# GLA's decayed queries by one product and a spread over heads on Pool, and matmul operands at multiples of 512 bytes

## Chip, core and metric

The kernel runs on one core of a Trainium2 chip. The metric is the device time of one execution in microseconds, the median of several runs. PE is TensorE (PEld its weight load), DVE VectorE, ACT ScalarE, POOL GpSimd and SP the engine whose queue issues the DMAs.

## What is computed

One step of a streaming encoder layer in float32: 64 tokens of a running stream, 16 learned meta tokens and 2048 new tokens, model width 1024. The reference, cut:

```
h = rms_norm(x);  proj = h @ w_in
aq, ak, av, lx, lg, gq, gk, gv, glr, gog = split(proj)
o = concat[diff_attention(aq, ak, av), rg_lru(lx, lg), gla(gq, gk, gv, glr, gog)] @ w_out;  x = x + o
h = rms_norm(x);  x = x + (gelu(causal_dwconv3(h @ w_up)) * (h @ w_gate)) @ w_down
y = rms_norm(x)
```

The gated linear attention (GLA) has 4 heads with 32 key and 64 value channels. In blocks of tokens it needs, for every pair i >= j of a block,

```
att[i, j] = sum_d q[i, d] * k[j, d] * exp(b[i, d] - b[j, d])        # b: running sum of the log gates
```

## The kernel before

**Products.** The big products run as three float32r products: operand and weight are each split into a rounded part and a remainder (h, l), and hi·hi, lo·hi and hi·lo are summed in PSUM. So a product over 1024 rows is 8 k steps of three matmuls, 24 in all. A weight piece is a tile of 128x1024: DMA'd into `raw` (two buffers), rounded by ACT into `whi` (L151), the remainder `wlo` made by Pool (L257) for two in three and by DVE (L157) for the rest (three buffers of each); the split pieces are stored in HBM (`WS`) and loaded again by later groups.

**Stages.** A tile scheduler orders each engine's instructions by its own simulated times and by priorities that the code sets; a generator that yields costs (`yield 800`) is one strand, and `flow` weaves the strands. Up to about 2035 us these strands run woven: `win` (the input projection over six blocks of columns, up to 384 tokens each; L641 with weights standing, L643 with tokens standing), `attention` (scores L1052 and L1059, row maximum `NB` on DVE L1061, exp `pc` on ACT L1062, mixing on Pool L154 and DVE L1100, transposes L1151, values L1166), `recurrent` (the RG-LRU and GLA, chunk by chunk: first the 64 + 16 tokens, then eight chunks of 256), and the first two FFN groups of 512 columns. From about 1888 us the second FFN group is alone. Stage three, from about 2035 us, is the third FFN group with column blocks of 336, 256 and 512: the output projection (L1434), `up_gate` (products `pu` and `pg`, L1299, for 22 tiles of the hidden width), and `down` (`pd`, L1366) after every four tiles, a "quad".

**A GLA level.** Within a block of 128 tokens the decay matrix is built in levels of half lengths m = 64, 32, ..., 1 (`level(li, m)`, seven a chunk, six in the first: 62). Per level, for all 128 key channels of the four heads by n = 256 tokens (128 in the first chunk): DVE makes the exponents in the tile EK (L878, L879), ACT the exp (L880, written E in the code), Pool the decayed keys kl = k * E in the second half of EK (L882), and DVE the decayed queries of the second halves (L886): four products of 32 channels by 128 tokens, each into its head's block of the block diagonal tile BD (128 x 4 x 128). There are two BD tiles per chunk, zeroed by Pool when the chunk starts (L864) and used in turn. PE multiplies kl by BD for each of the chunk's two groups of 128 tokens (L891), DVE copies the result under a mask into `att` (L895). `att` starts as the diagonal, set by Pool (L154, att<-ident,dg). EK, BD and other working tiles come from one ring of nine tiles of 2 KB (`rc`, NRC = 9).

**Addresses.** Offsets in bytes of a partition: the weight tiles lie at 16928, 21024 and 25120 (`whi`) and 29216, 33312 and 37408 (`wlo`), each 32 past a multiple of 512. The token tiles of `win` and of FFN groups 0 and 1 also lie 32 past a multiple of 512 (h2h of group 0 at 41504). In stage three the H tiles lie 480 past one: h2h of the 336-column block at 158688, of 256 columns at 180192, of 512 columns at 196576. One k step of H is 4n bytes, 1344 for n = 336. A gated tile `gh` or `gl` holds the three blocks one after the other, 1104 columns, 4416 bytes; their starts lie at odd multiples of 32.

The matmul of L1299, with H on the moving side and the weights standing:

```
for k in range(KT):
    for i3, (wi_, hx) in enumerate(((0, hk), (0, lk), (1, hk))):
        nc.tensor.matmul(ps[:, :n], lhsT=w_[wi_][:, k * P:(k + 1) * P], rhs=hx, ...)
```

Of the kernel before, what the change touches and what calls it, by code (L numbers as in the profile page):

```python
# [21 lines left out]
P = 128  # L22
# [113 lines left out]
def tile_hymba_step(ctx, tc, xT, xkT, cache_v, wi, wo, wu, wg, wd, par, sgla, c_msk, yT_p, yT_s, nkT_p, nv_p, lh_p, lc_p, gs_p, fc_p,  # L136
# [61 lines left out]
    lrue = cst.tile([P, 16], F32, name="lrue")  # L198
    halo = cst.tile([P, NF, 2], F32, name="halo")
    fce = cst.tile([P, 2, 2, NF], F32, name="fce")  # L200

    def pr(name, i=0, n=1):
        a = PAR[name][0] + i
# [579 lines left out]
    def gla(c):  # L783
# [75 lines left out]
        yield 1200  # L859

        att = [rc("att", (P, 4, P)) for _ in range(nb)]
        Bs = [rc("BD", (P, 4, P)) for _ in range(2)]
        for B_ in Bs:
            nc.gpsimd.memset(B_[:, :, :n // 2], 0.0)  # L864
        for j in range(nb):
            for h in range(4):
                pool_scaled(att[j][:, h, :], ident, dg[:, j, h:h + 1])
# [1 line left out]

        def level(li, m):  # L870
            cn = n // (2 * m)
            B_ = Bs[li % 2]
            bv = b[:, :n].rearrange("p (c t) -> p c t", t=2 * m)
            EK = rc("EK")
            E, kl = EK[:, 0, :], EK[:, 1, :]
            ew = E[:, :n].rearrange("p (c t) -> p c t", t=2 * m)
            ref = bv[:, :, m - 1:m].to_broadcast([P, cn, m])
            nc.vector.tensor_tensor(ew[:, :, 0:m], ref, bv[:, :, 0:m], ALU.subtract)  # L878
            nc.vector.tensor_tensor(ew[:, :, m:], bv[:, :, m:], ref, ALU.subtract)  # L879
            nc.scalar.activation(out=E[:, :n], in_=E[:, :n], func=AF.Exp, scale=1.0 / 16)  # L880
            yield 800
            nc.gpsimd.tensor_tensor(out=kl[:, :n], in0=k[:, :n], in1=E[:, :n], op=ALU.mult)  # L882
            qv = q[:, :n].rearrange("p (c t) -> p c t", t=2 * m)
            for h in range(4):
                r = slice(32 * h, 32 * h + 32)
                nc.vector.tensor_tensor(B_[r, h, :n // 2].rearrange("p (c t) -> p c t", t=m), qv[r, :, m:], ew[r, :, m:],  # L886
                                        ALU.mult)
            yield 800
            for j in range(nb):
                ps = half_bank().rearrange("p (h c) -> p h c", c=64)  # L890
                nc.tensor.matmul(ps, lhsT=kl[:, j * P:(j + 1) * P], rhs=B_[:, :, j * 64:(j + 1) * 64], start=True, stop=True)  # L891
                cc = P // (2 * m)
                ov = att[j].rearrange("p h (c t) -> p h c t", t=2 * m)[:, :, :, m:]
                mv = msk[:, li, :].rearrange("p (o c t) -> p o c t", o=1, t=m).to_broadcast([P, 4, cc, m])
                nc.vector.copy_predicated(out=ov, mask=mv, data=ps.rearrange("p h (c t) -> p h c t", t=m))  # L895
                yield 500
# [361 lines left out]
    def open3():  # L1258
        env["hs"].close()
        env["dg"], env["rg"] = "dg", "rg"  # L1260
        env["ps"] = p2.enter_context(tc.tile_pool(name="ps_x", bufs=5, space=PSUM))

        env["hp"] = p2.enter_context(tc.tile_pool(name="hp3", bufs=1, side="right"))
        env["xp"] = [p2.enter_context(tc.tile_pool(name="xp3", bufs=4, side="right")),
                     p2.enter_context(tc.tile_pool(name="xp4", bufs=4))]
        env["ev"] = p2.enter_context(tc.tile_pool(name="ev3", bufs=2))
        env["gp"] = p2.enter_context(tc.tile_pool(name="gp3", bufs=5))

    x2 = {}
# [6 lines left out]
    def up_gate(g, ff, H, gt, norms):  # L1276
        (wu_,), (wg_,) = w_take(("up", g, ff), 1), w_take(("gate", g, ff), 1)
        ev2, gp = env["ev"], env["gp"]
        gw = sum(FGROUPS[g])
        gh = gp.tile([P, gw], F32R, tag="gh", name="gh")  # L1280
        gl = gp.tile([P, gw], F32R, tag="gl", name="gl")
        gt[ff] = (gh, gl)
        cw = [pr("fcw", 22 * w + ff) for w in range(3)]
        cb = pr("fcb", ff)
        goff = 0
        for bi, n in enumerate(FGROUPS[g]):
            yield from norms.pop(bi, ())
            us = []
            for a, b, kind in ffn_pieces(g, n):
# [42 lines left out]
            for a, b, kind, uh, cc in us:  # L1332
# [5 lines left out]
                gh_, gl_ = gh[:, goff + a:goff + b], gl[:, goff + a:goff + b]  # L1338
                pool_scaled(gh_, cc[:, :m])
                minus(gl_, cc[:, :m], f(gh_))  # L1340
            goff += n
        w_used(2)

    def offsets(g):
        return [sum(FGROUPS[g][:b]) for b in range(len(FGROUPS[g]))]

    def down(g, q, gt, done=None, outs={}):
# [8 lines left out]
        for i, (ct, b) in enumerate(order):  # L1356
            half = ct // 4
            if half not in W:
                W[half] = w_take(("down", g, q, half), len(gts) // 2)
            o, n = offsets(g)[b], FGROUPS[g][b]  # L1360
            ps = env["ps"].tile([P, NMAX], F32, tag="w", name="pd")
            for j, (gh, gl) in enumerate(gts):
                c = j % 2 * NMAX + ct % 4 * P
                wh, wl = (a[:, c:c + P] for a in W[half][j // 2])
                for i3, (g_, w_) in enumerate(((gh, wh), (gh, wl), (gl, wh))):
                    nc.tensor.matmul(ps[:, :n], lhsT=w_, rhs=g_[:, o:o + n], start=(j == 0 and i3 == 0),  # L1366
                                     stop=(j == len(gts) - 1 and i3 == 2))
                if j % 2:
                    w_pump()
                    yield 6 * n * 0.425  # L1370
                    yield from beside(outs)
            nc.vector.tensor_tensor(x2[b, ct], x2[b, ct], ps[:, :n], ALU.add)  # L1372
            if done:
                done(b, ct)
            if all(c // 4 != half for c, _ in order[i + 1:]):
                w_used(len(gts) // 2)
# [258 lines left out]
```

## Time and profile before

| what | value |
|---|---|
| median of 3 runs | 2956.35 us (2955.74 to 2959.2) |
| profiled execution | 2957.12 us, its span 2955.3 us |
| PE busy | 2841.2 us, 96% |
| DVE busy | 1890.9 us, 64% |
| ACT busy | 1138.1 us, 39% |
| POOL busy | 870.5 us, 29% |
| mean granted clock of PE | 0.982 |

A matmul is in the trace with its modelled end, so the time that one takes in a stream is read from start to start, or from the chain of work, which gives runs of matmuls of one line as one piece. The shares are means over very unlike stretches; the windows tell them apart.

### The profile page before, as it was taken

Reading aid. Unit: us, or ns where it says so; the run is one execution under the profiler, and the core shown is the slowest. Engines: PE = TensorE matmul, PEld = TensorE weight load, DVE = VectorE, ACT = ScalarE, POOL = GpSimd, SP = SyncE. Lnnn points to the kernel's source line nnn. Section 1 sums busy time; section 2 is a strip of 40 time slices with the busy share of each in tenths; the row PEclk is TensorE's granted clock in tenths of the full one; section 3 lists DMA queues with packets and bytes.
Section 4 is the critical chain, followed back from the end, with each engine's and each line's share of the span. In section 5 each row is a group of like instructions: output and inputs, shape, how many; then the busy total and the mean of one; then the engine's idle time right before and its main releaser. Section 6 shows DMA issues by size and latency. Waiting matters only on the chain.

```text
span 2955.3 us, 44538 instructions
## 1 busy us (share of the span) xinstructions
PE 2841.2 (96%) x16031; PEld 2508.7 (85%) x16031; DVE 1890.9 (64%) x3699; ACT 1138.1 (39%) x2589; POOL 870.5 (29%) x1212
## 2 busy tenths in 40 slices
PE   7999999999898998999999999999999999999997
PEld 7988899989876887787787888888989998999997
DVE  7677685778879879879969865333454333333335
ACT  5354554555555454545445433211222121212122
POOL 4435534434535445444424221000110000000001
PEclk9999999999999999999999999999999999999999
DMA  7675564656796776777875565685222222222222
GB/s 241 201 217 148 179 214 139 199 179 186 227 338 212 252 264 234 249 266 261 285 258 183 197 203 183 208 327 186 72 86 86 86 86 86 86 86 86 86 86 105
DMA packets 277930, 537.43 MB, mean 182 GB/s; under 512 B 31014, under 2 KB 170030, under 8 KB 277710
## 3 DMA queue, kind: packets, MB, share of 16 engines
q1 hardware_dynamic: 277566, 534.58, 54.9%
q8 instruction: 127, 2.08, 0.3%
q14 instruction: 93, 0.76, 0.1%
q10 hardware_dynamic: 144, 0.01, 0.0%
HBM read 382.74 MB, written 151.76 MB: 181 GB/s over the span
## 4 chain that ended last, share of the span: by engine, by line
PE 69%; DVE 14%; DMA 4%; issue 2%; ACT 2%; POOL 1%; SPq 0%; POOLq 0%; ACTq 0%; DVEq 0%
PE pd L1366 15%; PE pg L1299 14%; PE pu L1299 14%; PE pd L1434 6%; PE ps_w L641 5%; PE ps_w L643 3%; DVE pc L1100 3%; PE ps_o L1166 3%; PE ps_sc L1059 2%; PE ps_pt L1151 2%; PE ps_sc L1052 2%; DVE BD L886 1%; DVE NB L1061 1%; PE ps_r L891 1%; DVE y L435 1%
## 5 line engine op out<-in xcount | busy, mean ns | idle before, releaser
L257 POOL TENSOR_TENSOR wlo<-raw,whi 128x1024 fp32r<-128x1024 f32 (+1 forms) x104 | 249.8, 2404 | 309.6 <-ACT whi L151 278.5
L1062 ACT ACTIVATE pc<-ps_sc,NB 128x512 f32<-128x512 f32 (+6 forms) x400 | 224.5, 562 | 298.2 <-DVE NB L1061 262.6
L1299 PE MATMUL pu<-h2h,whi 128*128 128x512 f32 (+2 forms) x880 | 316.8, 360 | 5.0 <-ACT h2h L151 2.8
L1323 DVE SCALAR_TENSOR_TENSOR cc<-uh,prm,cc 128x512 f32<-128x512 f32 (+4 forms) x264 | 165.0, 634 | 242.9 <-ACT cc L1321 239.8
L1299 PE MATMUL pu<-h2l,whi 128*128 128x512 f32 (+2 forms) x880 | 316.2, 359 | 1.4 <-DVE h2l L157 1.4
L1299 PE MATMUL pu<-h2h,wlo 128*128 128x512 f32 (+2 forms) x880 | 316.5, 360 | 0.0
L1366 PE MATMUL pd<-gh,whi 128*128 128x512 f32 (+2 forms) x880 | 314.2, 360 | 2.1 <-DMA whi<-WS 1.4
L1299 PE MATMUL pg<-h2h,wlo 128*128 128x512 f32 (+2 forms) x880 | 315.6, 359 | 0.4 <-DMA wlo<-WS 0.4
L1299 PE MATMUL pg<-h2l,whi 128*128 128x512 f32 (+2 forms) x880 | 315.9, 359 | 0.0
L1299 PE MATMUL pg<-h2h,whi 128*128 128x512 f32 (+2 forms) x880 | 315.0, 358 | 0.7 <-DMA whi<-WS 0.5
L1366 PE MATMUL pd<-gh,wlo 128*128 128x512 f32 (+2 forms) x880 | 314.5, 358 | 0.0
L1366 PE MATMUL pd<-gl,whi 128*128 128x512 f32 (+2 forms) x880 | 312.9, 357 | 0.0
L1372 DVE TENSOR_TENSOR x<-x,pd 128x512 f32<-128x512 f32 (+2 forms) x240 | 141.8, 595 | 217.1 <-PE pd L1366 216.1
L641 PE MATMUL ps_w<-hh,whi 128*128 128x384 f32 (+2 forms) x768 | 259.1, 340 | 16.0 <-ACT whi L151 10.5
L1316 ACT ACTIVATE uh<-pu 128x336 f32<-128x336 f32 (+3 forms) x132 | 59.3, 464 | 539.6 <-PE pu L1299 539.1
L1061 DVE TENSOR_REDUCE NB<-ps_sc 128x1 f32<-128x512 f32 (+6 forms) x400 | 209.5, 529 | 86.8 <-PE ps_sc L1059 85.2
L641 PE MATMUL ps_w<-hl,whi 128*128 128x384 f32 (+2 forms) x768 | 259.6, 339 | 0.4 <-DVE hl L157 0.4
L641 PE MATMUL ps_w<-hh,wlo 128*128 128x384 f32 (+2 forms) x768 | 256.0, 335 | 0.3 <-DVE wlo L157 0.3
L154 POOL TENSOR_SCALAR gh<-cc 128x336 fp32r<-128x336 f32 (+3 forms) x132 | 72.9, 553 | 444.8 <-DVE cc L1336 440.0
L151 ACT ACTIVATE whi<-raw 128x1024 fp32r<-128x1024 f32 (+2 forms) x160 | 165.8, 1036 | 96.7 <-DMA raw<-in_wi 30.5
L1299 PEld LDWEIGHTS pu<-h2h,whi 128*128 128x128 f32 x880 | 167.4, 190 | 26.6 <-ACT h2h L151 3.2
L154 POOL TENSOR_SCALAR pc<-pc,fr 128x512 f32<-128x512 f32 (+4 forms) x200 | 156.8, 802 | 109.3 <-DVE fr L1082 86.1
(330 smaller groups left out, 7142.5 us busy)
## 6 DMA issues: line engine op xcount, KB each, us to landing
whi<-WS SPq DMA_DIRECT2D x148, 512.0 KB, 4.3
wlo<-WS SPq DMA_DIRECT2D x148, 512.0 KB, 4.3
raw<-in_wi SPq DMA_DIRECT2D x74, 512.0 KB, 4.1
WS<-whi SPq DMA_DIRECT2D x74, 512.0 KB, 3.1
WS<-wlo SPq DMA_DIRECT2D x74, 512.0 KB, 6.0
Kc<-KHL SPq DMA_DIRECT2D x48, 512.0 KB, 5.8
V<-VHL SPq DMA_DIRECT2D x48, 512.0 KB, 3.5
Q<-QHL SPq DMA_DIRECT2D x64, 256.0 KB, 4.4
```

What stands on the lines that cost most here:

```text
L151: nc.scalar.activation(out=out, in_=in_, func=AF.Copy, scale=scale)
L154: nc.gpsimd.tensor_scalar(out, in_, s, 1.0, ALU.mult, ALU.mult)
L257: nc.gpsimd.tensor_tensor(out=lo[:, :n], in0=t[:, :n], in1=f(hi[:, :n]), op=ALU.subtract)
L641: nc.tensor.matmul(ps[:, :n], lhsT=wx, rhs=hx, start=st_, stop=sp_)
L643: nc.tensor.matmul(ps[:n, :wd_], lhsT=hx, rhs=wx, start=st_, stop=sp_)
L1061: nc.vector.tensor_reduce(NB[:qw, ti, m, ci:ci + 1], ps[:qw, :kt_], AX.X, ALU.min)
L1062: nc.scalar.activation(out=pv_[m][:qw, :kt_], in_=ps[:qw, :kt_], func=AF.Exp, scale=-1.0, bias=NB[:qw, ti, m, ci:ci + 1], accum_out=SS[:qw ...
L1299: nc.tensor.matmul(ps[:, :n], lhsT=w_[wi_][:, k * P:(k + 1) * P], rhs=hx, start=(k == 0 and i3 == 0), stop=(k == KT - 1 and i3 == 2))
L1323: nc.vector.scalar_tensor_tensor(out=cc[:, :m], in0=uh[:, w:w + m], scalar=cw[w], in1=cc[:, :m], op0=ALU.mult, op1=ALU.add)
L1366: nc.tensor.matmul(ps[:, :n], lhsT=w_, rhs=g_[:, o:o + n], start=(j == 0 and i3 == 0), stop=(j == len(gts) - 1 and i3 == 2))
L1372: nc.vector.tensor_tensor(x2[b, ct], x2[b, ct], ps[:, :n], ALU.add)
L1434: nc.tensor.matmul(ps[:, :n], lhsT=w_, rhs=g_, start=(k == 0 and i3 == 0), stop=(k == KT - 1 and i3 == 2))
```

## The change

**GLA levels.** The two BD tiles of a chunk and their zeroing go. Each level takes two more tiles from the `rc` ring: `qe`, the decayed queries of all 128 channels by 128 tokens in one DVE product, and BD, which Pool writes whole: qe, repeated over the four heads, times the head indicator of the channel (`hind`, four columns of `prm`), 128x512 with the zeros among it. EK's lines shift by three: L878 is now L875, L879 L876, L882 L879, L886 becomes L883 (DVE) and L886 (Pool), L891 L890; L257 is L258.

**Addresses.** A tile of 480 bytes (`pad0`) in front of the weights moves them and what lies behind by 480: weights and the H tiles of FFN groups 0 and 1 then begin at multiples of 512. In stage three a pad of 480 bytes on the right side brings the three H pairs to multiples of 512 (158208, 179712, 196096 for h2h), and one of 64 on the left with gated tiles of 1152 columns does it for gh and gl; `places` puts their blocks largest first at multiples of 128 columns (512 at 0, 336 at 512, 256 at 896). Of the 336-column H only each eighth k step lies at a multiple of 512, as 1344 is none.

```diff
+    nc.gpsimd.memset(cst.tile([P, 120], F32, name="pad0"), 0.0)
...
         att = [rc("att", (P, 4, P)) for _ in range(nb)]
-        Bs = [rc("BD", (P, 4, P)) for _ in range(2)]
-        for B_ in Bs:
-            nc.gpsimd.memset(B_[:, :, :n // 2], 0.0)
...
-            B_ = Bs[li % 2]
...
             nc.gpsimd.tensor_tensor(out=kl[:, :n], in0=k[:, :n], in1=E[:, :n], op=ALU.mult)
             qv = q[:, :n].rearrange("p (c t) -> p c t", t=2 * m)
-            for h in range(4):
-                r = slice(32 * h, 32 * h + 32)
-                nc.vector.tensor_tensor(B_[r, h, :n // 2].rearrange("p (c t) -> p c t", t=m), qv[r, :, m:], ew[r, :, m:],
-                                        ALU.mult)
+
+            qe, B_ = rc("qe", (P, P))[:, :n // 2], rc("BD", (P, 4, P))
+            nc.vector.tensor_tensor(qe.rearrange("p (c t) -> p c t", t=m), qv[:, :, m:], ew[:, :, m:], ALU.mult)
+            qb = qe.rearrange("p (o c) -> p o c", o=1).to_broadcast([P, 4, n // 2])
+            hb = pr("hind", 0, 4).rearrange("p (h o) -> p h o", o=1).to_broadcast([P, 4, n // 2])
+            nc.gpsimd.tensor_tensor(out=B_[:, :, :n // 2], in0=qb, in1=hb, op=ALU.mult)
             yield 800
...
+        pad(p2.enter_context(tc.tile_pool(name="pad_r", bufs=1, side="right")), 480)
         env["hp"] = p2.enter_context(tc.tile_pool(name="hp3", bufs=1, side="right"))
...
+        pad(p2.enter_context(tc.tile_pool(name="pad_l", bufs=1)), 64)
         env["gp"] = p2.enter_context(tc.tile_pool(name="gp3", bufs=5))
...
-        gw = sum(FGROUPS[g])
+        at, gw = places(g)
...
-        goff = 0
         for bi, n in enumerate(FGROUPS[g]):
+            goff = at[bi]
...
-            goff += n
         w_used(2)
+
+    def places(g):
+
+        at, n = {}, 0
+        for b in sorted(range(len(FGROUPS[g])), key=lambda b: -FGROUPS[g][b]):
+            at[b] = n
+            n += -(-FGROUPS[g][b] // P) * P
+        return at, n
+
+    def pad(pool, n):
+        nc.gpsimd.memset(pool.tile([P, n // 4], F32, tag="pad", name="pad", bufs=1), 0.0)
...
-            o, n = offsets(g)[b], FGROUPS[g][b]
+            o, n = places(g)[0][b], FGROUPS[g][b]
```

**Order.** The scheduler weaves the part up to stage three anew: PE carries out the same matmuls, some 5000 of them at another place, the level's matmuls at most some 60 places away. From stage three's first `down` product on PE's order is the same. On Pool, where the seventh chunk's levels begin, the order before was (the line of each instruction, its operation, output<-inputs, partitions x elements; uh, fce and halo belong to the FFN's convolution):

```order
L154 TENSOR_SCALAR att<-ident,dg 128x128 x8
L882 TENSOR_TENSOR EK<-qk,EK 128x256 x2
L257 TENSOR_TENSOR wlo<-raw,whi 128x1024
L882 TENSOR_TENSOR EK<-qk,EK 128x256
L257 TENSOR_TENSOR wlo<-raw,whi 128x1024
L1318 COPY fce<-uh 128x2
L1320 COPY halo<-uh 128x2
L882 TENSOR_TENSOR EK<-qk,EK 128x256
```

Now, on Pool at the same place (pc<-pc,fr scales attention's exponentials):

```order
L154 TENSOR_SCALAR att<-ident,dg 128x128 x8
L879 TENSOR_TENSOR EK<-qk,EK 128x256
L258 TENSOR_TENSOR wlo<-raw,whi 128x1024
L154 TENSOR_SCALAR pc<-pc,fr 128x512 x4
L154 TENSOR_SCALAR pc<-pc,fr 128x384 x2
L154 TENSOR_SCALAR pc<-pc,fr 128x16
L154 TENSOR_SCALAR pc<-pc,fr 128x144
L886 TENSOR_TENSOR BD<-qe,prm 128x512
L879 TENSOR_TENSOR EK<-qk,EK 128x256
L258 TENSOR_TENSOR wlo<-raw,whi 128x1024
L1319 COPY fce<-uh 128x2
L1321 COPY halo<-uh 128x2
```

Between the first level's kl and its BD there are now a weight split and eight scalings; the second level's kl comes behind that BD.

On DVE, where the fifth chunk's levels begin (738 us in the trace of before), the order before was (NB is the row maximum of attention, pl a remainder of its probabilities, msk the level's mask):

```order
L878 TENSOR_TENSOR EK<-bl 128x2x64
L879 TENSOR_TENSOR EK<-bl 128x2x64
L878 TENSOR_TENSOR EK<-bl 128x4x32
L879 TENSOR_TENSOR EK<-bl 128x4x32
L886 TENSOR_TENSOR BD<-qk,EK 32x128 x8
L1061 TENSOR_REDUCE NB<-ps_sc 128x1 x2
L157 TENSOR_TENSOR pl<-ps_pt,ph 128x512
L895 COPY_PREDICATED att<-msk,ps_r 128x4x64
```

Now, on DVE at the same place:

```order
L875 TENSOR_TENSOR EK<-bl 128x2x64
L876 TENSOR_TENSOR EK<-bl 128x2x64
L883 TENSOR_TENSOR qe<-qk,EK 128x128
L875 TENSOR_TENSOR EK<-bl 128x4x32
L876 TENSOR_TENSOR EK<-bl 128x4x32
L1060 TENSOR_REDUCE NB<-ps_sc 128x1 x2
L157 TENSOR_TENSOR pl<-ps_pt,ph 128x256
L883 TENSOR_TENSOR qe<-qk,EK 128x128
L1060 TENSOR_REDUCE NB<-ps_sc 128x1 x2
L157 TENSOR_TENSOR pl<-ps_pt,ph 16x256
L894 COPY_PREDICATED att<-msk,ps_r 128x4x64
```

The eight products of two levels have become two, each behind its own level's exponents, with attention's row maxima between them.

## Rows read from the trace of the kernel before

**Rows 1.** Windows: busy time of each engine by stretch; first row: columns.

```profile
core 0: us, PE busy (x) PEld busy (x) DVE busy (x) ACT busy (x) POOL busy (x), PEclk, DMA share, GB/s
...
100.00:900.00 800.00, 758.18 (x4831) 703.55 (x4830) 603.80 (x1236) 408.24 (x1020) 334.11 (x378) 0.98 0.66 203
900.00:1888.00 988.00, 954.33 (x4740) 788.17 (x4739) 790.44 (x1540) 462.82 (x1077) 381.83 (x507) 0.98 0.69 231
...
2146.00:2938.00 792.00, 790.42 (x4670) 718.36 (x4670) 315.50 (x570) 158.01 (x287) 65.83 (x202) 1.00 0.24 85
```

**Rows 2.** Waits: who waited <- releaser: us in total, times, longest us.

```profile
PE ps_sc L1052 <- ACT pc L1062: 22.4, 24, 3.5
...
PE ps_r L891 <- POOL EK L882: 0.4, 1, 0.4
PE ps_r L891 <- DVE BD L886: 0.4, 1, 0.4
...
ACT pc L1062 <- DVE NB L1061: 262.6, 174, 8.1
```

**Rows 3.** Chain of work, FFN group 1 alone: start us, us, what, matmuls.

```profile
1902.77 5.44 PE pu L1299 x24
```

**Rows 4.** Chain of work, stage three, 2146 to 2890 us.

```profile
2172.00 5.60 PE pu L1299 x24
...
2183.20 3.71 PE pu L1299 x24
...
2193.35 2.72 PE pg L1299 x24
...
2262.79 2.83 PE pu L1299 x24
...
2474.25 33.38 PE pd L1366 x204
...
2507.78 14.84 PE pd L1366 x84
```

**Rows 5.** Chain of work, projection stage, 440 to 480 us.

```profile
447.47 4.16 PE ps_w L641 x24
```

**Rows 6.** Groups by line and shape: out<-in, xcount | busy us, mean ns | idle before.

```profile
L257 POOL TENSOR_TENSOR wlo<-raw,whi 128x1024 fp32r<-128x1024 f32 x96 | 234.7, 2446 | 297.5 <-ACT whi L151 270.4 <-PE ps_w L643 7.4 <-issue 7.2
L886 DVE TENSOR_TENSOR BD<-qk,EK 32x128 f32<-32x128 f32 x224 | 104.0, 464 | 8.3 <-ACT EK L880 5.6
L154 POOL TENSOR_SCALAR pc<-pc,fr 128x512 f32<-128x512 f32 x96 | 85.4, 906 | 73.7 <-DVE fr L1082 71.2 <-PE ps_w L641 1.3 <-DVE dg L858 1.0
...
L879 DVE TENSOR_TENSOR EK<-bl 128x128 f32<-128x128 f32 x56 | 19.0, 340 | 0.0
...
L740 POOL TENSOR_TENSOR rc<-rc,sq 128x512 f32<-128x512 f32 x8 | 11.7, 1468 | 50.9 <-DVE tt L738 25.6 <-ACT lgt L749 16.2 <-issue 7.3
L940 POOL TENSOR_TENSOR oS<-oS,gss 128x512 f32<-128x512 f32 x8 | 8.8, 1097 | 0.5
...
L886 DVE TENSOR_TENSOR BD<-qk,EK 32x64 f32<-32x64 f32 x24 | 6.6, 275 | 1.7 <-ACT EK L880 1.3
```

**Rows 7.** All instructions of L886: duration ns min/median/max, first and last start.

```profile
L886 DVE TENSOR_TENSOR BD<-qk,EK x248: 212/288/2489, 100.0 to 1683.2; 32x128 f32<-32x128 f32 x112, 32x64 f32<-32x64 f32 x12
```

**Rows 8.** Timeline, a first and an ordinary level: start us, us, engine, what.

```profile
741.02 1.44 POOL L882 TENSOR_TENSOR EK<-qk,EK 128x256 f32<-128x256 f32 x2
741.84 0.70 PE L891 MATMUL ps_r<-BD,EK 128*128 128x256 f32 x2 [0.36 <-POOL EK L882]
...
1432.66 1.62 DVE L886 TENSOR_TENSOR BD<-qk,EK 32x128 f32<-32x128 f32 x4
1432.71 0.83 POOL L882 TENSOR_TENSOR EK<-qk,EK 128x256 f32<-128x256 f32 x1 [2.88 <-ACT EK L880]
...
1446.49 0.59 PE L891 MATMUL ps_r<-BD,EK 128*128 128x256 f32 x2
```

## Prediction

> **What bounds the kernel now.** I read the windows by stage first. Two kinds of stretch stand apart [rows 1]. From 2146 to 2938 us PE is busy for 790.4 of 792 us at a granted clock of 1.00, DVE for 40% and Pool for 8%: there the time is the number of matmuls times their spacing, and nothing that DVE or Pool does can show. From 100 to 1888 us (input projection, attention and recurrence woven with the first FFN groups) PE stands still for 41.8 + 33.7 = 75.5 us while DVE is busy for 603.8 + 790.4 = 1394.2 us, 78%. So the change has to be judged twice: by spacing in stage three, by waiting before it.
>
> The list of waits says whose fault the idle time of the mixed part is [rows 2]: the longest entry of PE is 22.4 us ahead of attention scores, for a bank that ACT's exp (L1062) frees; ACT in turn waited 262.6 us for DVE's row maximum (L1061). So DVE's load is felt, but thinly. The level that the change rewrites barely shows: PE waited once, 0.4 us, for BD and once, 0.4 us, for kl.
>
> Then the chain of work, for the spacing. All big products here are 24 matmuls, eight k steps by three splits. In FFN group 1 alone (1888 to 2035 us) a 512-column product takes 5.44 us [rows 3], 226.7 ns a matmul; 14 of 15 such rows say 5.44. In stage three the same code with the same 512 columns takes 5.60 us, 233.4 ns (36 rows of 5.60, three each of 5.59 and 5.61) [rows 4]. Clock and shape are the same. What differs in the program is where the operands lie: in group 1 H and weights both begin 32 bytes past a multiple of 512, in stage three the 512-column H begins 480 past one and the weights 32 past. The 256-column products, also at 480 against 32, take 2.83 us in 35 of 41 rows and 2.72 us in the other six, so 113.3 ns can be had there too, and it is half of 226.7: I call these two the floor. By columns the floor of 336 is 226.7 x 336/512 = 148.8 ns, 3.57 us a product; the row says 3.71. Against the address as the cause speaks the projection stage: H and weights both 32 past a multiple, and a 384-column product takes 4.16 us [rows 5] where the floor is 226.7 x 384/512 x 24 = 4.08.
>
> **The change, part by part.** The sum is made against the profiled execution's 2957.12 us; the median of the runs is 0.8 us lower.
>
> *Addresses in stage three.* After the change H of the 512- and 256-column blocks, the weights and the start of each gh and gl block lie on multiples of 512. 512 columns: 22 tiles of up and gate are 44 products, and the output projection has 8 more, 52 x (5.60 - 5.44) = 8.3 us. 256 columns: 44 products of which 35 in 41 are slow, 44 x 35/41 x 0.11 = 4.1 us. 336 columns: each k step is 1344 bytes on, so seven of eight H operands stay off a multiple; I take 0, with 44 x 0.14 = 6.2 us as the other end. Down: a full quad is 33.38 + 14.84 = 48.22 us for 288 matmuls [rows 4]; at the floor it is 96 x 1104/512 x 226.7 ns = 46.9 us, so 1.3 us by 5.5 quads, 7.2 us at most. Its old gh addresses ran over all odd multiples of 32, some of them as the weights', and I saw no faster quads there; I take half, 3.6, ends 0 and 7.2. Together 16.0 us, ends 0 (the address does nothing) and 25.8. A loss in this part has nothing to rest on: PE's order from the first down product of stage three on is the same and no operand gets further from a multiple.
>
> The Trainium skill ("TensorE: Matmul & The Clock Gate", Back-to-back issue gap) gives the spacing at full clock as columns over 2.4 GHz plus about 2.5 ns, 216 for 512, with no term for where an operand lies. By that rule this part is worth 0 and the first rival holds. The trace disagrees at least on the size: 226.7 and 233.4 ns for one shape at one clock [rows 3, 4].
>
> *Addresses before stage three.* FFN groups 0 and 1 go from 32 against 32 to 0 against 0; attention's operands don't move. I take 0. If the win products fell to the floor, 64 of 384 columns would give 64 x 0.08 = 5 us.
>
> *DVE.* Out go 224 products of 32x128 and 24 of 32x64, 104.0 + 6.6 = 110.6 us [rows 6]. In come 56 of 128x128, 340 ns by L879's row, and six of half the size at about half, 20.0 us; L886's 464 ns against 340 for four times the rows also shows that a DVE product costs by columns, not partitions. Net -90.6 us, 6.5% of 1394.2. The same share of 75.5 us of PE idle is 4.9, I take 5. Ends: the whole of the 22.4 us that PE waits for exp as the gain, and a loss of 12 us from the next item.
>
> *Pool.* Out go 18 memsets. In come 62 products, BD from qe and the head columns, 56 of them 128x512: between 1.10 us (L940, also with a broadcast operand) and 1.47 (L740) [rows 6], 65 to 87 us with the six of half the size; I take the first, nearest in shape. Pool was busy 334.1 + 381.8 of 1788 us, 40%, and goes to about 44%: room, but in a queue that runs in order. Each level now runs exp, then DVE's qe beside Pool's kl (0.83 us), then BD on Pool, where DVE made BD in 1.62 us beside kl [rows 8]. So BD is ready 0.83 + 1.10 - 1.62 = 0.3 us later, and more where something stands between kl and BD on Pool: nothing in 24 of 62 levels; a wlo split (2.45 us) alone or with scalings of attention in most others; in the seventh chunk's first level, quoted above, a split and eight scalings, 2.45 + 4 x 0.91 + about 1.7 by columns for the other four = 8 us. Queued behind BD on Pool are the next kl, wlo (for which the projection's third split waits) and the scalings of attention. Cover: in an ordinary level BD was ready at 1434.28 us and its matmul ran at 1446.49, 12.2 us later. In a chunk's first level Pool's two kl end at 742.46 and PE's two matmuls at 742.54; nothing covers it. Of the eight first levels behind the first chunk's, five have nothing or a two-column copy on Pool in between (0.3 us each), the last two a gh scaling (about 1 us each), the seventh chunk's the 8: about 12 us, if PE stands for all of it, which is the loss above. The three pad memsets stand at tile set-up, away from PE's chain. The BD and qe tiles come from the rc ring of nine, three a level where one was: a level's tiles must be free before the third next begins, which the order on DVE gives anyway; 0.
>
> The Trainium skill ("SBUF — State Buffer", SBUF: two separate sides) says that DVE with two SBUF inputs and GpSimd lock one port pair for a whole instruction and that the loser blocks. The trace agrees: one BD product took 2489 ns where the median is 288 [rows 7], about one wlo split. By that rule 62 new Pool holds of 1.1 us would block DVE for up to 68 us and eat most of its 90; the mixed term would be 1 in place of 5 and the time 2940.
>
> *Sum:* 2957.1 - 16.0 - 5 = 2936 us; with the address worth between half of it, 8, and all, 25.8, it is 2944 to 2926.
>
> **Rivals.**
> *B, the address does nothing*, and 5.44 against 5.60 is something else that sets in with stage three (the 256-column products change between 2.72 and 2.83 at unchanged addresses, and 384 columns miss the floor when aligned: both speak for it; against it, that nearly all 512-column rows of a place agree to 0.01 us, as a fixed cause would make them). Only DVE's 5 us stay: 2952.
> *C, every product falls to the floor*, 336 columns and all of down too, since the weights count by themselves: 25.8 + 5 in the projection + 5 = 35.8, 2921. For it: all shapes of stage three are above the floor by much the same 5 to 7 ns, 336 too, whose addresses vary. Against: rows 5.
> *D, slower: Pool becomes what PE waits for in each chunk's opening levels.* The seventh chunk's opening is one of eight; if each chunk's second level, which has a split between kl and BD in half of them, is uncovered too, a split and a dear BD, 2.45 + 1.47 = 3.9 us at each of eight chunks, 31 us, stand on PE. With 16 of stage three kept: 2957.1 + 31 - 16 = 2972. It decides when PE's wait ahead of the level matmuls passes (16 + 6)/62 = 0.35 us a level on the mean; today it is 0.8 us for all [rows 2], and in most levels 12 us lie between. The new order on Pool speaks for it.
> *E, the re-woven mixed part loses what stage three gains.* About 5000 rows of PE's order stand elsewhere before stage three; 12 us of new waits among 75.5 of old ones would be enough: 2957.1 + 12 - 16 = 2953.
>
> **How the numbers follow.** Forecast 0.45, B 0.18, C 0.12, D 0.14, E 0.11. A measurement of this kernel can tell about 0.2%, 5.9 us. Faster, under 2950.4: the forecast, C, 0.06 of B, 0.04 of E: 0.67. Within: 0.11 of B, 0.05 of E, 0.03 of D: 0.19. Slower: 0.11 of D, 0.02 of E, 0.01 of B: 0.14. The range goes from C with a larger share of exp's 22.4 us, 2912, to E and B with a few us of new waits, 2958; left out are most of D and the low end of C, about 2 in 10.
>
> **What would show it.** In the chain of stage three 512-column products at 5.44 and 256-column ones at 2.72 throughout, 336 at 3.71 still, a full quad of down between 46.9 and 48.2 us. B is shown by 5.60 unchanged, C by 3.57 and 46.9. In the windows from 100 to 1888 us DVE should lose about 90 us of busy time, Pool gain 56 to 80, PE's idle fall by about 5. D is shown by waits of PE, L890 on Pool's BD, of tens of us; E by PE idle above 80 us with other releasers. The forecast is wrong if stage three changes by less than 8 us, or if the mixed part moves by more than 12 either way.

## The result, and the profile after

The changed kernel takes 2933.64 us (median of 4 runs, 2929.76 to 2936.13) where the kernel before, timed beside it, takes 2957.77 (2955.74 to 2960.65): ratio 0.9917, 95% interval 0.9899 to 0.9934, some 24 us. The forecast was 2936. The total came as predicted, its two parts did not: the addresses gave a quarter of what was forecast for them, the part ahead of stage three nearly four times what was forecast for it. The two errors cancel, and that is luck.

Where the time went is read best from one place that both programs have: the long row of output projection matmuls that opens stage three. In the chain of work of the kernel before (start us, us, what, matmuls):

```profile
2036.13 75.97 PE pd L1434 x463
```

and of the changed kernel, with the rows that answer to [rows 4]:

```profile
2017.29 75.74 PE pd L1445 x463
...
2220.51 2.87 PE pu L1300 x24
...
2226.27 5.47 PE pu L1300 x24
2231.73 5.44 PE pg L1300 x24
2237.17 3.71 PE pu L1300 x24
...
2309.39 33.39 PE pd L1377 x204
...
2342.94 14.81 PE pd L1377 x84
```

Stage three starts 18.8 us earlier. From that row to the end of the span it took 2955.3 - 2036.1 = 919.2 us and takes 2932.7 - 2017.3 = 915.4, 3.8 less. The 512-column products fell from 5.60 to 5.47 (up) and 5.44 (gate), as forecast; the 256-column ones rose from 2.72 or 2.83 to 2.87, which was not; 336 columns and down are as before.

The part ahead, in the windows up to that row (columns as in [rows 1]). Before:

```profile
100.00:2036.00 1936.00, 1858.33 (x10227) 1612.28 (x10227) 1445.99 (x2855) 896.04 (x2135) 728.42 (x926) 0.98 0.69 223
```

After:

```profile
100.00:2017.00 1917.00, 1851.97 (x10226) 1603.09 (x10224) 1397.24 (x2669) 894.34 (x2136) 782.03 (x974) 0.98 0.69 225
```

The same matmuls: PE's idle time falls from 77.7 to 65.0 us, its busy time by 6.4 (its granted clock is taken up with the load put back, below). DVE loses 48.8 us, not 90; Pool gains 53.6.

The groups by line and shape say why DVE lost only half (columns as in [rows 6]; first L878 of the kernel before, which is now L875, then the changed kernel):

```profile
L878 DVE TENSOR_TENSOR EK<-bl 128x128 f32<-128x128 f32 x56 | 20.3, 363 | 0.0
...
L886 POOL TENSOR_TENSOR BD<-qe,prm 128x512 f32<-128x512 f32 x56 | 63.0, 1125 | 68.0 <-PE ps_r L890 64.0 <-DVE qe L883 3.2 <-DVE pc L1099 0.8
...
L883 DVE TENSOR_TENSOR qe<-qk,EK 128x128 f32<-128x128 f32 x56 | 39.3, 702 | 14.1 <-ACT EK L877 8.0 <-POOL BD L886 5.8
L875 DVE TENSOR_TENSOR EK<-bl 128x128 f32<-128x128 f32 x56 | 38.1, 681 | 0.0
```

qe takes 702 ns where 340 was taken for it, and the first exponent product, which the change does not touch, 681 where it took 363. The timeline shows what they stand behind, and what an exponent product takes by itself (start us, us, engine, what):

```profile
279.36 1.04 POOL L886 TENSOR_TENSOR BD<-qe,prm 128x512 f32<-128x512 f32 x1 [1.46 <-PE ps_r L890]
279.64 0.91 DVE L875 TENSOR_TENSOR EK<-bl 128x128 f32<-128x128 f32 x1
...
280.47 0.28 DVE L876 TENSOR_TENSOR EK<-bl 128x128 f32<-128x128 f32 x1
...
1169.99 2.38 POOL L258 TENSOR_TENSOR wlo<-raw,whi 128x1024 fp32r<-128x1024 f32 x1
1170.04 2.49 DVE L883 TENSOR_TENSOR qe<-qk,EK 128x128 f32<-128x128 f32 x1
```

Both DVE products end some 0.15 us behind the Pool instruction during which they started: 280.55 against 280.40, 1172.53 against 1172.37. This is the port lock of the Trainium skill ("SBUF — State Buffer", SBUF: two separate sides). The trace agrees with it for Pool's kl, BD and weight splits, behind which 66 of the 70 qe and exponent products that started during one ended by 0.08 to 0.16 us; beside Pool's products with one scalar (L154) 21 of 36 ended first, a qe at 562.84 us in 0.31 us for one, and there the lock does not show. In these two groups, qe and L875, what they take more than was taken for them is 56 x (0.36 + 0.32) = 38 us, most of the 42 by which DVE's relief fell short.

Not all of it is new. qe stands mostly behind kl, which Pool made before too: 30 started during a kl and took 0.71 us on the mean, seven during a weight split, none during a BD. The exponents stand behind BD: 23 started during one and took 0.87 us, six during a split. The four old products of a level were held as well, with a mean of 464 ns against a median of 288 [rows 7]. At 0.28 us each, L878 and L886 of before were 87 us of work in 134 us of busy time, L875 and L883 now are 35 in 81: 47 us held before, 46 after. DVE was spared the work of three products in four, some 52 us, and none of the holding.

The waits of the changed kernel (who waited <- releaser: us, times, longest):

```profile
ACT pc L1061 <- DVE NB L1060: 198.8, 150, 6.0
POOL BD L886 <- PE ps_r L890: 64.0, 19, 8.2
PE ps_sc L1051 <- ACT pc L1061: 17.3, 19, 4.1
...
PE ps_o L1165 <- DVE pl L157: 3.3, 6, 1.1
...
PE ps_r L890 <- DVE att L894: 1.7, 3, 1.1
```

Against [rows 2]: ACT waits 63.8 us less for the row maximum, PE 5.1 less for exp. PE's wait for pl, a remainder of attention that DVE makes, was 8.2 us and is 3.3. PE's list names neither BD nor kl. New are the 64.0 us that Pool waits for PE, ahead of BD: its tile in the ring is free only when an older level's matmul has run.

### The profile page after: what moved, and what is told of

It is laid out like the page before. It is cut to its first block, busy times and chain, and to the rows that moved or that the text cites. A ratio compares the mean times of both kernels' runs of the same rounds, so it can differ in the third digit from the quotient of the medians.

```text
span 2932.7 us, 44448 instructions
## 1 busy us (share of the span) xinstructions
PE 2829.0 (96%) x16031; PEld 2500.8 (85%) x16031; DVE 1841.8 (63%) x3513; ACT 1136.6 (39%) x2589; POOL 923.5 (31%) x1259
## 4 chain that ended last, share of the span: by engine, by line
PE 71%; DVE 12%; DMA 8%; issue 3%; ACT 2%; POOL 2%; SPq 1%; POOLq 0%; ACTq 0%; DVEq 0%
PE pd L1377 15%; PE pg L1300 15%; PE pu L1300 15%; PE ps_w L642 7%; PE pd L1445 5%; PE ps_o L1165 3%; PE ps_w L644 3%; DMA Q<-QHL 2%; PE ps_sc L1058 2%; PE ps_pt L1150 2%; PE ps_sc L1051 2%; DVE pc L1099 1%; PE ps_r L890 1%; DVE NB L1060 1%; DVE y L436 1%
## 5 line engine op out<-in xcount | busy, mean ns | idle before, releaser
L258 POOL TENSOR_TENSOR wlo<-raw,whi 128x1024 fp32r<-128x1024 f32 (+1 forms) x104 | 250.6, 2410 | 245.9 <-ACT whi L151 227.4
L642 PE MATMUL ps_w<-hh,whi 128*128 128x384 f32 (+2 forms) x768 | 258.8, 339 | 16.4 <-ACT whi L151 10.5
L154 POOL TENSOR_SCALAR gh<-cc 128x336 fp32r<-128x336 f32 (+3 forms) x132 | 73.2, 554 | 449.9 <-DVE cc L1337 428.8
L154 POOL TENSOR_SCALAR pc<-pc,fr 128x512 f32<-128x512 f32 (+4 forms) x200 | 162.4, 830 | 119.5 <-DVE fr L1081 105.0
L1377 PEld LDWEIGHTS pd<-gh,whi 128*128 128x128 f32 x880 | 166.2, 189 | 27.4 <-DVE x L1383 4.9
```

Of the source, the lines that this page charges most:

```text
L154: nc.gpsimd.tensor_scalar(out, in_, s, 1.0, ALU.mult, ALU.mult)
L258: nc.gpsimd.tensor_tensor(out=lo[:, :n], in0=t[:, :n], in1=f(hi[:, :n]), op=ALU.subtract)
L642: nc.tensor.matmul(ps[:, :n], lhsT=wx, rhs=hx, start=st_, stop=sp_)
```

## The experiments

Times are compared as ratios to the kernel before, run beside them. The part ahead is read as the start of the output projection's row (2036.1 before, 2017.3 after), stage three from there to the end. The start of that row differs from run to run: four kernels that share the code ahead and the weights' addresses, the changed one among them, started it at 2008.6, 2010.1, 2014.7 and 2017.3. Differences of 5 us there say nothing; spacings in stage three repeat to 0.01 us. TensorE's granted clock goes with part of that spread: between 100 us and the row it stood at the lower of its two levels, 1.2 GHz, for 47.8, 51.2, 54.6 and 61.4 us in these four, by the traces' clock records.

### Levels alone

The changed kernel without `pad0`, the two pads and `places`; PE's order is that of after.

```diff
-    nc.gpsimd.memset(cst.tile([P, 120], F32, name="pad0"), 0.0)
...
-        pad(p2.enter_context(tc.tile_pool(name="pad_r", bufs=1, side="right")), 480)
...
-        pad(p2.enter_context(tc.tile_pool(name="pad_l", bufs=1)), 64)
...
-        at, gw = places(g)
+        at, gw = offsets(g), sum(FGROUPS[g])
```

> The change without its addresses: the levels are computed as after (one product on DVE, the spread on Pool, tiles from the ring), all operands lie where they lay before, and PE's order is that of after. After the change the long row of the output projection in the chain starts at 2017 us where it started at 2036, and stage three is some 4 us shorter. If the 19 us in front come from the levels (DVE relieved, or the new weave that goes with it), this kernel starts that row at about 2017 and takes about 2939 us, with 512-column products at 5.60 us. If they come from the weights' addresses, the row starts near 2036 and the time is about 2957.

Ratio 0.9953 (0.9937 to 0.9970), 14 us. The chain:

```profile
2018.52 75.97 PE pd L1431 x463
...
2253.38 5.60 PE pu L1297 x24
```

The row starts 17.6 us earlier than before with every old address: the gain ahead belongs to the levels. Stage three is as before, 921.0 us.

### Addresses alone

The changed kernel with the levels of before; PE's order is that of before.

```diff
+        Bs = [rc("BD", (P, 4, P)) for _ in range(2)]
...
+            B_ = Bs[li % 2]
...
-            qe, B_ = rc("qe", (P, P))[:, :n // 2], rc("BD", (P, 4, P))
...
+            for h in range(4):
+                r = slice(32 * h, 32 * h + 32)
+                nc.vector.tensor_tensor(B_[r, h, :n // 2].rearrange("p (c t) -> p c t", t=m), qv[r, :, m:], ew[r, :, m:],
+                                        ALU.mult)
```

> The change without its levels: addresses as after, levels as before, and PE's order is that of before. If the addresses act in stage three alone: the part ahead as before (row of the output projection at 2036 us), 512-column products at 5.44 to 5.47 us in place of 5.60, 256-column ones at 2.87, together 4 us less, about 2953. If they also shorten the part ahead: about 2934 to 2945. If they do nothing by themselves: 2957.

Ratio 0.9987 (0.9973 to 1.0001), 4 us, at the edge of what can be told. The row starts at 2042.26 in its profile, which is of the slowest of its twelve executions (2958.87 us, granted clock 0.976); stage three takes 914.8 us, with the products of after:

```profile
2245.01 2.87 PE pu L1302 x24
...
2250.76 5.47 PE pu L1302 x24
2256.23 5.44 PE pg L1302 x24
```

So the addresses act in stage three alone here, by some 4 us. The two parts apart give 14 + 4 = 18 us; together 24. The intervals are wide enough for that. Whether the weights' new addresses also help the new weave ahead is open: with it, three profiles with weights at 32 began stage three at 2018.5, 2020.3 and 2021.8, four with weights at 0 at 2008.6 to 2017.3 (the three stood at 1.2 GHz for 58.0, 64.8 and 68.3 us ahead of it, the four for 47.8 to 61.4, so part of that can be clock); with the old weave they helped nothing. The spacings ahead did not move: a 512-column product of FFN group 1 takes 5.44 us and 23 projection matmuls of 384 columns 3.99 before and after.

### The spread on DVE

```diff
-            nc.gpsimd.tensor_tensor(out=B_[:, :, :n // 2], in0=qb, in1=hb, op=ALU.mult)
+            nc.vector.tensor_tensor(B_[:, :, :n // 2], qb, hb, ALU.mult)
```

> The change with the spread of qe over the heads (128x512) made by DVE in place of Pool, all else as after; the weave becomes a third one. DVE's relief is then some 90 us less 62 spreads of about 0.6 us, so some 50 us; Pool has no new work and no new wait. If the gain ahead of stage three goes with DVE's load, some 10 of the 19 us are left, about 2943. If Pool's new wait (64 us in 19 stops ahead of BD after the change) costs time, this kernel is faster than after, under 2930. If the weave alone decides, any time from 2930 to 2955.

Ratio 0.9941 (0.9922 to 0.9960), row at 2016.89. DVE is busy 1405.2 us up to 2017, 8 more than after: it makes 62 more products, but its others are held up less (qe 437 ns, L875 461). The interval overlaps that of after: on which engine the spread stands is worth too little to tell here, and with DVE's load nearly that of after the cases of the expectation cannot be told apart. What the two groups of rows suggest is that DVE gets back in blocking much of what it is spared in work.

### DVE's load put back

qe is made five times over, with the same values.

```diff
             nc.vector.tensor_tensor(qe.rearrange("p (c t) -> p c t", t=m), qv[:, :, m:], ew[:, :, m:], ALU.mult)
+            for h in range(4):
+                nc.vector.tensor_tensor(qe.rearrange("p (c t) -> p c t", t=m), qv[:, :, m:], ew[:, :, m:], ALU.mult)
```

> As after, but DVE makes each qe five times over (four more products of 128x128 a level, same values), so that DVE's load in front of stage three is no longer relieved: 248 products of some 0.34 to 0.44 us, 85 to 110 us more than after, when DVE lost 49 us by the change. Pool's work is as after; the weave is another one. If the 19 us in front of stage three come from DVE's relief, they go and more: the long row of the output projection starts at 2036 us or later, the time is about 2955 or above, and ACT's wait for the row maximum is back above 260 us. If the weave or the Pool part made them, the row stays near 2017 and the time near 2937.

Ratio 0.9965 (0.9952 to 0.9979). The row starts at 2026.56. The window up to it, and the wait of ACT:

```profile
100.00:2027.00 1927.00, 1853.45 (x10238) 1605.98 (x10237) 1464.33 (x2922) 894.97 (x2137) 788.46 (x974) 0.98 0.68 224
...
ACT pc L1063 <- DVE NB L1062: 232.6, 163, 5.6
```

DVE now carries 1464 us, 18 more than before the change, and ACT's wait is half way back. By the profiles 9.3 of the 18.8 us ahead are lost; by the ratios 0.9965 - 0.9917, 14 us of some 20. Both cases of the expectation missed: the row is neither at 2036 nor near 2017. So DVE busier than before leaves 6 to 10 us of the gain, and load is not the only cause. Nor is the loss that of load alone, for the four products also stand between qe and BD and lengthen each level's own chain:

```profile
PE ps_sc L1053 <- ACT pc L1063: 9.4, 11, 1.8
...
PE ps_r L892 <- DVE att L896: 7.9, 5, 2.8
...
PE ps_r L892 <- POOL BD L888: 2.6, 2, 1.6
```

PE's waits for att and BD are 10.5 us where the changed kernel had 1.7, and its wait for exp, the path that the forecast went by, fell from 17.3 to 9.4 although ACT's wait for the row maximum rose. So what PE pays did not follow ACT's wait here.

TensorE's granted clock is another part of what the levels brought. The mean over the span, before, after, and with the load put back:

```profile
core 0: 2955.3 us, clock 0.982
...
core 0: 2932.7 us, clock 0.985
...
core 0: 2942.2 us, clock 0.985
```

By the clock records PE stood at 1.2 in place of 2.4 GHz for 78.5 us between 100 us and the row before, 61.4 after and 61.4 with the load put back. The 512-column products there are spaced 427 ns in place of 227, so 17 us less are worth up to some 8 us, an estimate: of the order of the fall in PE's busy time (6.4 us after, 4.9 here) and of what the load left. The higher clock goes with the levels, not with the addresses: every execution on record of the kernel before was granted 0.976 to 0.984 and those of the addresses alone 0.976 to 0.985, those of the levels alone 0.982 to 0.987 and of the changed kernel 0.984 to 0.986. What kept it up no run isolates, nor do these runs separate the new weave from the place of the level's products among attention's row maxima on DVE.

### Tiles of its own for BD and qe

```diff
-    NPC, NRC, NW, NRAW, NSQ = 9, 9, 3, 2, 3
+    NPC, NRC, NW, NRAW, NSQ = 9, 7, 3, 2, 3
...
-            qe, B_ = rc("qe", (P, P))[:, :n // 2], rc("BD", (P, 4, P))
+            qe, B_ = mp.tile([P, P], F32, tag="qe", name="qe", bufs=2)[:, :n // 2], mp.tile([P, 4, P], F32, tag="BD", name="BD", bufs=2)
```

> As after, with BD and qe in tiles of their own (two each) in place of three tiles a level from the shared ring, which has seven tiles in place of nine. After the change Pool stood 64 us in 19 stops ahead of BD until PE's level matmul had freed a tile. If that new wait is paid on PE (weight splits and scalings of attention queue behind it), this kernel is faster than after by some of it, 2925 or less. If it is idle time of an engine that has room, the time stays at 2930 to 2938. If two BD tiles are too few, the wait stays as it was.

Ratio 0.9893 (0.9879 to 0.9907). Pool's wait for PE ahead of BD is gone, and PE's for exp halves:

```profile
ACT pc L1061 <- DVE NB L1060: 214.4, 157, 7.0
...
PE ps_sc L1051 <- ACT pc L1061: 8.9, 13, 2.0
...
POOL BD L886 <- DVE qe L883: 4.2, 17, 0.4
```

The row starts at 2007.77; a kernel that keeps the ring (narrow H at 128 bytes, below), timed beside the same kernel before, started it at 2010.06. By its time, 2923.0, the first case holds, but the kernel before was 4 us faster beside it; against after the ratio is 0.0024 lower, 7 us, and the intervals overlap. So of 64 us of waiting at most some 7 were paid, and perhaps none.

### Weights at 32 bytes, H at multiples

```diff
-    nc.gpsimd.memset(cst.tile([P, 120], F32, name="pad0"), 0.0)
...
-        pad(p2.enter_context(tc.tile_pool(name="pad_l", bufs=1)), 64)
+        pad(p2.enter_context(tc.tile_pool(name="pad_l", bufs=1)), 32)
```

> The change with the weights and all that lies behind them on the left side back at 32 bytes past multiples of 512; H of stage three and the gated tiles stay at multiples of 512, and PE's order is that of after. If what counts is that H and weights lie at the same place modulo 512, the 512-column products go back to about 5.60 us and the time to about 2939. If H alone counts, they stay at 5.44 to 5.47 and the time at 2934.

Ratio 0.9963 (0.9949 to 0.9977), 2947 us where 2939 was expected; stage three takes 923.4 us, 8 more than after and 4 more than before the change, as the output projection's row (76.29 us) and a quad of down (48.49) are slower than in either:

```profile
2227.36 2.84 PE pu L1299 x24
...
2233.04 5.60 PE pu L1299 x24
```

H at multiples of 512 alone is worth nothing: 512 columns are back at 5.60.

### Both at 32 bytes, and H at 256

In the one for 256 only the right pad changes; in the one for 32, `pad0` is gone as well.

```diff
-        pad(p2.enter_context(tc.tile_pool(name="pad_r", bufs=1, side="right")), 480)
+        pad(p2.enter_context(tc.tile_pool(name="pad_r", bufs=1, side="right")), 224)
```

```diff
-    nc.gpsimd.memset(cst.tile([P, 120], F32, name="pad0"), 0.0)
...
-        pad(p2.enter_context(tc.tile_pool(name="pad_r", bufs=1, side="right")), 480)
+        pad(p2.enter_context(tc.tile_pool(name="pad_r", bufs=1, side="right")), 448)
```

> As after, with weights, the three H pairs and the gated tiles of stage three all 32 bytes past multiples of 512. If it is the same place modulo 512 that counts, the 512-column products stay at 5.44 to 5.47 us as after; if multiples of 512 are needed, they go back to 5.60 as where H lay at multiples and the weights 32 past.

> As after, with the three H pairs of stage three 256 bytes past multiples of 512, the weights at multiples. If the places have to agree modulo 512, the 512-column products go back to 5.60 us; if modulo 256 or a smaller power of two from 64 on is enough, they stay at 5.44 to 5.47.

Both at 32:

```profile
2229.70 5.47 PE pu L1299 x24
2235.17 5.44 PE pg L1299 x24
```

H at 256, weights at 0:

```profile
2241.46 5.47 PE pu L1300 x24
2246.93 5.44 PE pg L1300 x24
```

Multiples of 512 are not what counts. Wide products are at the floor where H and weights differ by 0 or 256, and at 5.60 where they differ by 448 (before) or 480 (weights at 32, H at 0). One execution each; the totals were 2938.3 and 2925.3 us beside 2951.6.

### 336 columns in rows of 384

```diff
-        H = h_tiles(FGROUPS[g], env["hp"], ("h2h", "h2l"))
+        H = [[t[:, :, :n] for t in h] for h, n in
+             zip(h_tiles([-(-n // P) * P for n in FGROUPS[g]], env["hp"], ("h2h", "h2l")), FGROUPS[g])]
```

> As after, with the 336-column H of stage three held in rows of 384 columns, so that its k steps are 1536 bytes apart and all eight lie at multiples of 512. Same instructions, same order. If a product is at the floor when H and weights lie at the same place modulo 512, the 336-column products go from 3.71 to 3.57 us, 44 x 0.14 = 6 us off stage three (915 us after the change, from the long row of the output projection to the end), and the 256-column products behind them may follow to 2.72. If columns, not places, set who is slow, 336 and 256 stay at 3.71 and 2.87.

One execution, 2930.5 us beside 2951.6. All operands now start alike:

```profile
2258.76 3.68 PE pu L1300 x24
...
2266.13 2.88 PE pu L1300 x24
```

3.68, not 3.57, and 256 columns stay at 2.88. The narrow products do not go by the rule of the wide ones.

### The blocks in another order

```diff
-FGROUPS = [[512], [512], [336, 256, 512]]
+FGROUPS = [[512], [512], [336, 512, 256]]
```

> As after, with the blocks of stage three in the order 336, 512, 256 in place of 336, 256, 512 (other tokens in the last two blocks, same sizes). In the trace of after a product seems to start as the one ahead ended: the 512-column products lose 16 cycles in the first matmuls behind a 256-column one and none later. If that is carried over, the 256-column products now stand behind a 512-column one that ended at the floor and take 2.72 us; the 512-column ones, behind 336, settle within a few matmuls. Stage three then loses 44 x 0.15 = 7 us of its 915. If 256 columns are slow by themselves, they stay at 2.87.

One execution, 2935.2 us beside 2951.6. Behind a 512-column product that runs at the floor, 256 columns still take 2.87:

```profile
2248.25 5.44 PE pg L1300 x24
2253.69 2.87 PE pu L1300 x24
```

What a product finds from the one ahead is thus worth a few matmuls (the 0.03 us between 5.47 and 5.44), not its rate.

### Narrow H at 128 and at 448 bytes

In the first the H tiles of 336 and 256 columns lie 128 bytes past multiples of 512 and the 336 is held in rows of 384. The second has 448 in place of 128 (a pad of 64) and the own tiles for BD and qe.

```diff
-        H = h_tiles(FGROUPS[g], env["hp"], ("h2h", "h2l"))
+        H = []
+        for bi, n in enumerate(FGROUPS[g]):
+            if bi == 2:
+                pad(env["hp"], 384)
+            H.append([env["hp"].tile([P, KT, -(-n // P) * P], F32R, tag=f"{tg}{bi}", name=f"{tg}{bi}", bufs=1)[:, :, :n]
+                      for tg in ("h2h", "h2l")])
```

> As after, with the H of the 336 and 256 columns of stage three 128 bytes past multiples of 512 (the 336 in rows of 384 columns, so all its k steps) and the H of 512 columns at multiples, weights at multiples. At equal places modulo 256 the 512-column products ran at the floor, but 256 columns took 2.87 to 2.88 and 336 in rows of 384 3.68; before, with H 448 past the weights, 256 columns took 2.72 or 2.83. If the narrow products want other places than the wide ones, they fall below 2.87 and 3.68 here; if 128 is as good as 0, they stay; the 512-column ones stay at 5.44 to 5.47 either way.

> The change with BD and qe in tiles of their own (two each, the ring of seven) and, in stage three, the H of 336 and 256 columns 448 bytes past multiples of 512 (the 336 in rows of 384 columns) with the H of 512 columns and the weights at multiples. With own tiles the part ahead ends at about 2008 us. If the narrow products keep what 448 bytes gave them before (2.72 or 2.83 us in place of 2.87) beside wide ones at the floor, stage three takes 912 to 915 us as against 915.4 after the change, and the whole about 2920. If each product starts in the state that the one ahead left, so that narrow ones at another place spoil the wide ones, the 512-column products go above 5.47 and stage three is not shorter than 915.

At 128 (one execution, 2924.8 us beside 2953.6):

```profile
2237.11 2.84 PE pu L1300 x24
...
2242.80 5.47 PE pu L1300 x24
...
2253.71 3.69 PE pu L1300 x24
```

At 448:

```profile
2247.56 3.75 PE pu L1300 x24
...
2255.05 2.75 PE pu L1300 x24
2257.80 2.72 PE pg L1300 x24
2260.51 5.46 PE pu L1300 x24
2265.97 5.44 PE pg L1300 x24
```

With 448 bytes between H and weights 256 columns reach the floor (16 of 20 gate products at 2.72, four at 2.83) beside wide ones at theirs, and 336 columns are at their slowest, 3.75. Stage three takes 2916.6 - 2005.8 = 910.8 us. The kernel takes 2920.59 us (2915.53 to 2924.95), ratio 0.9880 (0.9848 to 0.9911): the fastest of the study, below the changed kernel by its median, though the intervals touch.

## Why the prediction came out right, step by step

**What bounds it: right in the main.** Stage three goes by the spacing of matmuls, the part ahead by waits, and by the granted clock, which the forecast had no term for. By the signs that the prediction set itself it was wrong on both counts: stage three changed by less than 8 us and the mixed part by more than 12.

**Addresses in stage three, 16.0 us: wrong in size, 3.8.** 512 columns: forecast 5.44, measured 5.47 and 5.44, so 44 x 0.145 = 6.4 us of the 7.0 that up and gate had in the 8.3; the output projection gave 0.2 (75.97 to 75.74) in place of 1.3. 256 columns: forecast -4.1, measured 44 x (2.87 - 2.81) = +2.6 us, 2.81 being the mean of before's rows. 336: 0, as taken. Down: 48.22 before, 48.20 after, 0.1 in place of 3.6. The step that failed was taking the floor of one width for all. The rows spoke against it: at one place, 448 bytes apart, 256 columns reached 2.72 while 512 never left 5.60, and 384 columns missed the floor with places alike. I named the second and used it for a rival only. Taking half for down between ends of 0 and 7.2, where no quad at any old address had been faster, had no row behind it.

**Addresses ahead, 0: not contradicted,** and not settled (above).

**DVE, -90.6 us: -48.8.** The 340 ns for qe came from a product that mostly ran with Pool idle, and the 110.6 us taken out were a mean with some 40 us of holding in it, which came back in qe and the exponents. The rule of the port lock was weighed and priced at up to 68 us; 38 of the 42 us missing stand in the two held groups. For DVE's busy time the Trainium skill's rule was the nearer one, and the text gave it a sentence where it deserved the term.

**The gain ahead, 5 us: 18.8.** The step that failed is the proportion: DVE's share of relief applied to PE's idle time. Half the relief gave 12.6 us less idle and 6.4 less busy time of PE for the same matmuls. A queue that others wait on is no tax spread evenly. The load put back cost 9 to 14 us for 67 us of DVE, so one us of DVE was worth at most 0.14 to 0.21 us of the end, against 0.054 in the forecast; the rest came with the new levels in another way, the granted clock as part of it, and was not in the sum at all. The upper end, the whole 22.4 us of PE's wait for exp, did contain it.

**Pool, 12 us of loss in first levels: none.** PE's list of waits names neither BD nor kl, so the seventh chunk's eight scalings cost PE no wait there. The ring was put at 0 because the order on DVE would cover it; it made Pool wait 64 us, of which at most some 7 reached the end. Pool had the room for it; the reason given for the 0 was wrong.

**Rivals.** B is refuted for 512 columns by the weights moved back (5.60); 336 columns and down gained nothing here, but other places moved them too (3.68 to 3.75, a quad of 48.49). C is refuted: no place tried brings 336 to 3.57. D has no wait to show. E went the other way: the re-woven part gained.

So 2936 against 2933.6 is 12 us too much in one term and 14 too little in the other. The ends of the two terms, 25.8 and 22.4 us of gain, held both measured values.

## What to carry to other kernels

Read the spacing of each shape at each place before moving tiles: one width's best place can be another's worst, and what counted was the distance between moving operand and weights, not a round address. Work taken from a queue that others wait on can be worth several times its share of the idle time; put a dummy load back to measure it, beside the chain in question and not in it, and compare the granted clock too. Between VectorE and GpSimd, price a moved instruction on both: what VectorE hands over can hold up VectorE's other products from there. Take an instruction's work from rows where it ran undisturbed (0.28 us), not from a mean with waiting in it (0.46).

## What the runs showed of the hardware

For these float32r products at a granted clock of 1.00, by the distance of H from the weights modulo 512: 512 columns take 226.7 ns at 0 and 256, 233.4 at 448 and 480. 256 columns take 119.8 at 0 and 256, 118.5 at 128 and 480, 113.3 or 117.9 at 448. 336 columns take 153 to 156 at all places tried. The step between the two rates of the wide ones, 6.7 ns, is 16 cycles of 2.4 GHz. The mechanism is open, as is why 256 columns at 448 bytes run at either of two rates.

In the changed kernel 66 of 70 VectorE products of 128x128 or half of it that started during GpSimd's kl, BD or weight split ended some 0.15 us behind it: 0.91 us under a BD of 1.04, 2.49 under a split of 2.38, where such a product takes 0.28 alone. Made on VectorE, the 128x512 spread, 0.68 us alone, ended 0.55 us behind. Beside GpSimd's products of a tile with one scalar (L154) 21 of 36 ran through in some 0.3 us.
